# Attention of two heads at once in plain fp32 instead of one head at a time in split halves

## The chip, the cores and the metric

The kernel runs on one core of a Trainium2 chip, and the time is the device time of one execution in microseconds (us). A core has five engines with queues of their own: TensorE (PE in the profile: matrix multiplies; PEld are its weight loads, which run beside the multiplies), VectorE (DVE), ScalarE (ACT), GpSimd (POOL) and SyncE (SP, which issues most DMAs). They meet only through semaphores. Matrix products land in PSUM, eight banks of 128 partitions by 512 fp32 values.

## The reference

One decoder layer on a sequence of 512 tokens, model width 1024, all in float32: a norm, one wide input projection, a Mamba-2 scan over 16 heads and a forgetting attention over 16 heads side by side, an output projection, and a gated MLP. The change touches the attention alone:

```python
def fox_mixer(q, k, v, f_raw, f_bias, q_norm_w, k_norm_w):
    qh = rms_norm(heads(q), q_norm_w)          # 16 heads of 64
    kh = rms_norm(heads(k), k_norm_w)
    vh = heads(v)
    cum = jnp.cumsum(log_f, axis=1).transpose(0, 2, 1)
    for start in range(0, s, Q_BLOCK):         # blocks of 128 queries
        end = start + Q_BLOCK
        logits = jnp.einsum('bhqd,bhkd->bhqk', qh[:, :, start:end], kh[:, :, :end]) * scale
        logits = logits + cum[:, :, start:end, None] - cum[:, :, None, :end]
        p = jax.nn.softmax(jnp.where(causal, logits, -jnp.inf), axis=-1)
        outs.append(jnp.einsum('bhqk,bhkd->bhqd', p, vh[:, :, :end]))
```

## The kernel before

Large products keep fp32 accuracy by splitting: an operand is rounded to a type that TensorE takes in one pass (`F32R`, the "h" part), and what is left over is a second operand (the "l" part). `mm3` (L117) then adds three one-pass products, h·h, h·l and l·h. Rounding is an ACT copy (L110), the rest a DVE or POOL subtraction (L111). The input projections (rows named pw, pq, g), the output projection (po) and the MLP (up, Y, Z, X) are such products, and they are most of TensorE's work.

The attention works head by head, 16 heads of 64, as pairs of neighbouring heads that share the 128 columns of one transposed block.

- `v_proj` projects the values of four heads and keeps them split, 64 columns of h beside 64 columns of l (L533 on ACT, L534 on DVE).
- `fox_qk`, once for a pair, transposes q and k (L551). For each head it puts the h part of q over 64 partitions and the l part over the other 64 (`qs`); k gets its h part twice and its l part twice (`ks`), by ACT (L558) and DVE (L559). The copy on the other 64 partitions is made by ACT and DVE for the first pair (L561, L562) and by a DMA `ks<-ks` on SP's queue for the others.
- `fox_probs`, once for a head, fetches the row of cumulated gates by a DMA (`cum`), builds the bias with its causal mask in `bias` (ACT L584, POOL L586 and L589), and then for each of four query blocks adds two one-pass products over all 128 partitions (L599, L600; 128, 256, 384 and 512 columns), takes bias and row minimum in one DVE instruction (L601), the exponential on ACT (L605), and at the end scales the rows (L609).
- `fox_values`, once for a head, transposes the probabilities on TensorE in ten blocks (L626), splits them (ACT L628, DVE L629), and for each of four key blocks adds two one-pass products into one PSUM bank: h of the probabilities with all 128 columns of v, and l with 64 columns (L639). The two 64-partition halves of that bank are then added (ACT L643, DVE L644), and after a pair's second head the 128 rows are split for the output projection (L649, L650).

What sets the order: the loop at the end of the function calls these helpers head by head, with "fillers" between them (the projections of later heads and parts of the output projection). The attention's helpers run under `urgent()`, a priority that places their instructions early, and a scheduler puts the fillers' matmuls between them in each engine's queue. PSUM has three banks for the projections (`pg`), four for everything short-lived, scores and transposes included (`pm`), and one for the attention's output (`po`).

Of the kernel before, what the change touches and what calls it, by code (L numbers as in the profile page):

```python
# [15 lines left out]
P = 128  # L16
# [40 lines left out]
def tile_hybrid_layer(  # L57
# [468 lines left out]

    def v_proj(gi):
        tiles = token_block(wv[gi], "v%d" % gi)
        v = pa.tile([P, NTB, 4, 2 * HD], F32R, tag="v", name="v", bufs=2)
        for tb in range(NTB):  # L530
            c = (tb % 2) * 256
            o = tiles[tb // 2][:, c : c + 256].rearrange("p (h d) -> p h d", d=HD)
            act.activation(v[:, tb, :, 0:HD], o, AF.Copy, scale=r[:, tb : tb + 1])  # L533
            dve.scalar_tensor_tensor(  # L534
                out=v[:, tb, :, HD:], in0=o, scalar=r[:, tb : tb + 1], in1=raw(v[:, tb, :, 0:HD]),
                op0=ALU.mult, op1=ALU.subtract,
            )
        return v

    LO, HI = slice(0, HD), slice(HD, P)  # L540
    HALVES = ((LO, HI), (HI, LO))
    QOFF = (0, 128, 384, 768)

    def fox_qk(pair, tq, tk):
        qs = [pf.tile([P, SEQ], F32R, tag="qs", name="qs", bufs=4) for _ in range(2)]
        ks = [pf.tile([P, 2, SEQ], F32R, tag="ks", name="ks", bufs=4) for _ in range(2)]
        pr = pair % 2
        for tok, w in ((tk, kw), (tq, qw8)):
# [3 lines left out]
            for hd, (own, other) in enumerate(HALVES):  # L552
                src, sw = t[own, :], w[own]
                if tok is tq:
                    h, l = qs[hd][own, :], qs[hd][other, :]
                else:
                    h, l = ks[hd][own, 0, :], ks[hd][own, 1, :]
                act.activation(h, src, AF.Copy, scale=sw)  # L558
                dve.scalar_tensor_tensor(out=l, in0=src, scalar=sw, in1=raw(h), op0=ALU.mult, op1=ALU.subtract)  # L559
                if tok is tk and pair == 0:  # L560
                    act.activation(ks[hd][other, 0, :], src, AF.Copy, scale=sw)  # L561
                    dve.scalar_tensor_tensor(  # L562
                        out=ks[hd][other, 1, :], in0=src, scalar=sw, in1=raw(h), op0=ALU.mult, op1=ALU.subtract
                    )
                elif tok is tk:
                    nc.sync.dma_start(raw(ks[hd][other, :, :]), raw(ks[hd][own, :, :]))
        osum = pf.tile([P, SEQ], F32, tag="osum", name="osum", bufs=2)
        return qs, ks, osum

    def fox_probs(head, qs, ks):  # L570
# [4 lines left out]
        nm = pf.tile([P, NTB], F32, tag="nm", name="nm", bufs=2)  # L575
        sm = pf.tile([P, NTB], F32, tag="sm", name="sm", bufs=2)
        bias = pf.tile([P, 1280], F32, tag="bias", name="bias", bufs=2)
        prob = pf.tile([P, 1280], F32, tag="prob", name="prob", bufs=2)
        for qb in range(NTB):
            n = (qb + 1) * P  # L580
            b = bias[:, QOFF[qb] : QOFF[qb] + n]
# [7 lines left out]
            pool.affine_select(  # L589
                out=b[:, n - P :], in_=b[:, n - P :], pattern=[[-1, P]], compare_op=ALU.is_ge, fill=NEG, base=0,  # L590
                channel_multiplier=1,
            )
        for qb in range(NTB):
            n = (qb + 1) * P
            b = bias[:, QOFF[qb] : QOFF[qb] + n]
            p = prob[:, QOFF[qb] : QOFF[qb] + n]
            sps = mbank("S")
            qst = qs[:, qb * P : (qb + 1) * P]
            pe.matmul(sps[:, :n], qst, ks[:, 0, :n], start=True, stop=False)  # L599
            pe.matmul(sps[:, :n], qst, ks[:, 1, :n], start=False, stop=True)  # L600
            dve.tensor_tensor_reduce(  # L601
                out=p, in0=sps[:, :n], in1=b, scale=-1.0, scalar=-NEG, op0=ALU.add, op1=ALU.min,
                accum_out=nm[:, qb : qb + 1],
            )
            act.activation(p, p, AF.Exp, scale=-1.0, bias=nm[:, qb : qb + 1], accum_out=sm[:, qb : qb + 1])  # L605
        dve.reciprocal(sm, sm)
        for qb in range(NTB):
            p = prob[:, QOFF[qb] : QOFF[qb] + (qb + 1) * P]
            dve.tensor_scalar(out=p, in0=p, scalar1=sm[:, qb : qb + 1], scalar2=None, op0=ALU.mult)  # L609
        return prob  # L610

    def fox_values(head, prob, v, osum):
        lh = head % 4
        own, other = HALVES[head % 2]
        where = {}
        for n, kbs in enumerate(((0,), (1, 3), (2,))):
            w = sum(SEQ - kb * P for kb in kbs)
            t = mbank("pT")
            ph = pf.tile([P, w], F32R, tag="ph%d" % n, name="ph", bufs=2 if n == 0 else 1)
            pl = pf.tile([P, w], F32R, tag="pl%d" % n, name="pl", bufs=2 if n == 0 else 1)  # L620
            w = 0
            for kb in kbs:
                where[kb] = (ph, pl, w)
                for qb in range(kb, NTB):
                    o = QOFF[qb] + kb * P
                    pe.transpose(t[:, w : w + P], prob[:, o : o + P], ident)  # L626
                    w += P
            act.copy(ph, t[:, :w])  # L628
            dve.tensor_sub(pl, t[:, :w], raw(ph))  # L629
        o = po.tile([P, 512], F32, tag="o", name="o")  # L630
        for kb in range(NTB):
            ph, pl, w = where[kb]
            s = slice(w, w + SEQ - kb * P)
            cols = o[:, kb * P :]
            passes = ((P, slice(0, P), ph), (HD, slice(0, HD), pl))
            if kb == NTB - 1:
                passes = passes[::-1]
            for n, (m, vc, pt) in enumerate(passes):
                pe.matmul(  # L639
                    cols[:m], v[:, kb, lh, vc], pt[:, s], start=kb == 0 and n == 0, stop=kb == NTB - 1 and n == 1,  # L640
                    skip_group_check=True,
                )
        act.copy(osum[own, :], o[other, :])  # L643
        dve.tensor_add(osum[own, :], o[own, :], osum[own, :])  # L644
        if head % 2 == 0:
            return None
# [34 lines left out]
    def start_pair(p):  # L681
        with urgent():
            pairs[p] = fox_qk(p, *qk[p // 2])

    def start_head(n):
        qs, ks, _ = pairs[n // 2]
        with urgent():
            probs[n] = fox_probs(n, qs[n % 2], ks[n % 2])

    def end_head(n):  # L690
        with urgent():
            m = fox_values(n, probs.pop(n), vs[n // 4], pairs[n // 2][2])
        if m is not None:
            mf.append(m)

    fillers = {
        0: ["q1"], 3: ["v1"], 4: ["q2", "v2"], 5: ["o0"], 8: ["q3"], 9: ["a0", "o1"], 10: ["v3"], 12: ["o2"],
# [12 lines left out]
            out_proj((4 + g,), mf[2 * g : 2 * g + 2])  # L710

    start_pair(0)
    start_head(0)
    start_head(1)
    for n in range(16):
        for f in fillers.get(n, ()):
            fill(f)
        if n % 2 == 0 and n < 14:
            start_pair(n // 2 + 1)
        end_head(n)  # L720
        if n + 2 < 16:
            start_head(n + 2)
# [4 lines left out]
    nw = pf.tile([P, 1280], F32, tag="bias", name="nw", bufs=2)[:, :D]  # L727
    nc.sync.dma_start(nw, norm_ffn_w.to_broadcast([P, D]))
    for half in range(2):
        c = slice(half * 512, (half + 1) * 512)  # L730
        ks = slice(half * 4, half * 4 + 4)
        for tb in range(NTB):
            s = slice(tb * P, (tb + 1) * P)
            with urgent():
                xw = pf.tile([P, 512], F32, tag="osum" if tb % 2 else "cum", name="xw", bufs=2)
# [302 lines left out]
```

## Time and profile before

| what | value |
|---|---|
| timed runs | 805.68, 808.84, 808.51 us; median 808.51 |
| the profiled execution's own time | 806.18 us |
| its span | 804.4 us, granted TensorE clock 0.998 |
| DVE busy | 598.1 us (74%) |
| ACT busy | 438.6 us (55%) |
| POOL busy | 268.1 us (33%) |
| attention's stretch, first to last score and value product | about 221 to 438 us |

A row of the timeline gives the start, the duration, and with "x2" how many neighbouring instructions of one form were merged. TensorE works as a pipeline: a product lasts longer than the time until the next one starts. What a product costs a full queue is the step from its start to the next start, not its duration. `128*64` in a row is the number of rows and columns of the array that the product uses.

### The profile page before, as it was taken

What the parts mean: (1) busy time and instruction counts of PE and PEld (TensorE: products, weight loads), DVE (VectorE), ACT (ScalarE), POOL (GpSimd) and SP (SyncE); (2) the same over time, 40 slices, a digit from 0 to 9 for tenths busy, and PEclk for the clock granted to TensorE, in tenths of its full rate; (3) what the DMA queues carried; (4) which work ended last, traced back from release to release, by engine and by line L of the source; (5) the groups of instructions that cost most, each with busy time, mean ns of one, the idle gap of its engine ahead of it and who ended that gap; (6) DMA issues with size and microseconds to landing.
All of it is one profiled execution on the core that took longest, in us unless ns stands there. A gap on an engine that the chain in (4) does not pass through costs nothing.

```text
span 804.4 us, 11066 instructions
## 1 busy us (share of the span) xinstructions
PE 793.2 (99%) x3975; PEld 662.8 (82%) x3975; DVE 598.1 (74%) x949; ACT 438.6 (55%) x803; POOL 268.1 (33%) x266
## 2 busy tenths in 40 slices
PE   8999999999999999999999999999999999999997
PEld 6888877878989888888888888888888888888886
DVE  4797997588678789779796777667666766777744
ACT  7557645363588686685663554444443443556531
POOL 0004453643539147226310523333332233132120
PEclk9999999999999999999999999999999999999999
DMA  9615232331424243333330462232233233299983
GB/s 327 196 56 179 87 99 77 128 131 56 147 83 128 72 145 92 97 104 115 95 102 29 149 190 89 96 104 101 83 105 104 80 105 104 78 261 178 222 188 95
DMA packets 31399, 98.14 MB, mean 122 GB/s; under 512 B 4016, under 2 KB 5104, under 8 KB 31344
## 3 DMA queue, kind: packets, MB, share of 16 engines
q1 hardware_dynamic: 27456, 85.38, 32.1%
q0 software_dynamic: 3456, 11.54, 8.1%
q8 instruction: 31, 0.51, 0.3%
q10 hardware_dynamic: 432, 0.52, 0.2%
q14 instruction: 24, 0.20, 0.1%
HBM read 91.56 MB, written 2.20 MB: 117 GB/s over the span
## 4 chain that ended last, share of the span: by engine, by line
PE 89%; DVE 5%; DMA 2%; issue 2%; ACT 1%; POOL 1%; SPq 0%; DVEq 0%; POOLq 0%; ACTq 0%
PE up L117 30%; PE pw L117 15%; PE po L117 9%; PE Y L117 6%; PE g L117 5%; PE pq L117 4%; PE X L117 4%; PE Z L117 4%; PE o L639 2%; PE pT L626 2%; PE yd L458 2%; PE j L117 1%; PE S L600 1%; PE S L599 1%; DVE xs L397 1%
## 5 line engine op out<-in xcount | busy, mean ns | idle before, releaser
L110 ACT CAST wh<-wraw 128x1024 fp32r<-128x1024 f32 x103 | 108.2, 1052 | 121.6 <-PE up L117 79.3
L117 PE MATMUL up<-hh,wh 128*128 128x512 f32 (+1 forms) x360 | 138.6, 386 | 0.0
L117 PE MATMUL up<-hl,wh 128*128 128x512 f32 (+1 forms) x360 | 138.5, 385 | 0.0
L117 PE MATMUL up<-hh,wl 128*128 128x512 f32 (+1 forms) x360 | 138.3, 384 | 0.0
L111 DVE TENSOR_TENSOR wl<-wraw,wh 128x1024 fp32r<-128x1024 f32 x83 | 109.0, 1314 | 20.8 <-ACT wh L110 19.0
L117 PEld LDWEIGHTS up<-hl,wh 128*128 128x128 f32 x360 | 67.6, 188 | 13.7 <-issue 0.2
L117 PEld LDWEIGHTS up<-hh,wh 128*128 128x128 f32 x360 | 67.5, 188 | 13.6 <-issue 0.2
L117 PEld LDWEIGHTS up<-hh,wl 128*128 128x128 f32 x360 | 67.6, 188 | 13.3
L117 PE MATMUL pw<-wh,xh 128*128 128x512 f32 x192 | 77.3, 407 | 0.0
L117 PE MATMUL pw<-wl,xh 128*128 128x512 f32 x192 | 76.0, 396 | 0.0
L117 PE MATMUL pw<-wh,xl 128*128 128x512 f32 x192 | 75.8, 396 | 0.0
L831 DVE TENSOR_TENSOR up<-up,R 128x512 f32<-128x512 f32 x44 | 30.3, 692 | 59.5 <-PE up L117 59.5
L111 POOL TENSOR_TENSOR wl<-wraw,wh 128x1024 fp32r<-128x1024 f32 x20 | 50.2, 2511 | 60.9 <-ACT wh L110 60.9
L836 DVE SCALAR_TENSOR_TENSOR ua<-up,pc,ua 128x511 f32<-128x511 f32 (+1 forms) x88 | 66.3, 758 | 1.4
L605 ACT ACTIVATE prob<-prob,nm 128x384 f32<-128x384 f32 (+2 forms) x64 | 35.9, 562 | 29.3 <-DVE nm L601 29.2
L792 ACT CAST wh<-T 128x1024 fp32r<-128x1024 f32 (+1 forms) x30 | 29.3, 977 | 36.9 <-PE Z L117 15.3
L793 DVE TENSOR_TENSOR wl<-T,wh 128x1024 fp32r<-128x1024 f32 (+1 forms) x30 | 33.8, 1134 | 19.2 <-ACT wh L792 18.8
L586 POOL TENSOR_SCALAR bias<-cum,tokS 128x256 f32<-128x256 f32 (+1 forms) x32 | 21.4, 678 | 77.5 <-DVE nm L601 67.5
L846 POOL TENSOR_TENSOR ua<-ua 128x512 f32<-128x512 f32 x11 | 15.0, 1365 | 92.5 <-DVE ua L836 92.5
L117 PEld LDWEIGHTS pw<-wh,xh 128*128 128x128 f32 x192 | 36.1, 188 | 7.3 <-issue 0.5
L117 PEld LDWEIGHTS pw<-wl,xh 128*128 128x128 f32 x192 | 36.2, 188 | 7.2 <-issue 0.7
L117 PEld LDWEIGHTS pw<-wh,xl 128*128 128x128 f32 x192 | 36.0, 188 | 7.3
(241 smaller groups left out, 2004.3 us busy)
## 6 DMA issues: line engine op xcount, KB each, us to landing
wraw<-in_wup_dram SPq DMA_DIRECT2D x44, 512.0 KB, 3.3
T<-in_wdown_dram POOLq DMA_DIRECT2D x20, 512.0 KB, 7.7
wraw<-in_wqk_dram SPq DMA_DIRECT2D x16, 512.0 KB, 3.3
wraw<-in_wout_dram SPq DMA_DIRECT2D x16, 512.0 KB, 3.4
wraw<-in_wxbc_dram SPq DMA_DIRECT2D x11, 512.0 KB, 5.5
wraw<-in_wdown_dram SPq DMA_DIRECT2D x10, 512.0 KB, 3.6
T<-in_wdown_dram SPq DMA_DIRECT2D x10, 512.0 KB, 5.6
wraw<-in_wz_dram SPq DMA_DIRECT2D x8, 512.0 KB, 3.2
```

What stands on the lines that cost most here:

```text
L110: act.copy(h, r)
L111: (sub or dve).tensor_tensor(out=l, in0=r, in1=raw(h), op=ALU.subtract)
L117: ins = pe.matmul(o, a, b, start=start and n == 0, stop=stop and n == 2, **kw)
L458: pe.matmul(yd[:, h * HD : (h + 1) * HD], sc[:, h, :], xdt[:, h * HD : (h + 1) * HD], start=True, stop=True)
L586: pool.tensor_scalar(out=b, in0=cum[:, :n], scalar1=-1.0, scalar2=edge, op0=ALU.mult, op1=ALU.add)
L605: act.activation(p, p, AF.Exp, scale=-1.0, bias=nm[:, qb : qb + 1], accum_out=sm[:, qb : qb + 1])
L626: pe.transpose(t[:, w : w + P], prob[:, o : o + P], ident)
L639: pe.matmul(cols[:m], v[:, kb, lh, vc], pt[:, s], start=kb == 0 and n == 0, stop=kb == NTB - 1 and n == 1, skip_group_check=True,)
L792: act.copy(h[:, :n], src[:, :n])
L793: dve.tensor_tensor(out=l[:, :n], in0=src[:, :n], in1=raw(h[:, :n]), op=ALU.subtract)
L831: dve.tensor_mul(xp, o, R2)
L836: dve.scalar_tensor_tensor(out=a[:, s:], in0=xp[:, : SEQ - s], scalar=pc[:, cw + 2 - s : cw + 3 - s], in1=a[:, s:], op0=ALU.mult, op1=ALU.add,
```

## The change

Both heads of a pair are now worked on together, and nothing in the attention is split before its result. The values stay whole, 64 columns a head. `fox_qk` makes one fp32 tile of q and one of k, with the pair's first head on partitions 0 to 63 and its second on 64 to 127. `fox_bias` builds the bias inside the tile that later holds the probabilities. `fox_scores` issues for each query block one fp32 product of 64 rows for each head, into two banks. `fox_turn` transposes the probabilities and copies them once, unsplit. `fox_values` adds, for both heads, fp32 products of 64 columns into one bank, the first head on its partitions 0 to 63 and the second on 64 to 127. The loop starts a pair's scores for both heads in one step, turns each head in its place, and ends a pair after its second head. The core of the diff:

```diff
 def v_proj(gi):
-        v = pa.tile([P, NTB, 4, 2 * HD], F32R, tag="v", name="v", bufs=2)
...
-            dve.scalar_tensor_tensor(
-                out=v[:, tb, :, HD:], in0=o, scalar=r[:, tb : tb + 1], in1=raw(v[:, tb, :, 0:HD]),
+        v = pa.tile([P, NTB, 4, HD], F32, tag="v", name="v", bufs=2)
...
+                act.activation(v[:, tb], o, AF.Copy, scale=r[:, tb : tb + 1])
 def fox_qk(pair, tq, tk):
-        qs = [pf.tile([P, SEQ], F32R, tag="qs", name="qs", bufs=4) for _ in range(2)]
-        ks = [pf.tile([P, 2, SEQ], F32R, tag="ks", name="ks", bufs=4) for _ in range(2)]
...
-                elif tok is tk:
-                    nc.sync.dma_start(raw(ks[hd][other, :, :]), raw(ks[hd][own, :, :]))
+            f = pf.tile([P, SEQ], F32, tag=tag, name=tag, bufs=2)
+            act.activation(f, t, AF.Copy, scale=w)
+    def fox_scores(q, k, both):
...
+            sps = [mbank("S") for _ in range(2)]
+            for o, rows in zip(sps, HEADS):
+                pe.matmul(o[:, :n], q[rows, qb * P : (qb + 1) * P], k[rows, :n], start=True, stop=True)
-            pe.matmul(sps[:, :n], qst, ks[:, 0, :n], start=True, stop=False)
-            pe.matmul(sps[:, :n], qst, ks[:, 1, :n], start=False, stop=True)
...
-            act.copy(ph, t[:, :w])
-            dve.tensor_sub(pl, t[:, :w], raw(ph))
+            act.copy(pt, t[:, :w])
...
+            for i, rows in enumerate(HEADS):
+                pt, w = turned[i][kb]
                 pe.matmul(
-                    cols[:m], v[:, kb, lh, vc], pt[:, s], start=kb == 0 and n == 0, stop=kb == NTB - 1 and n == 1,
+                    o[rows, kb * P :], v[:, kb, (2 * pair + i) % 4, :], pt[:, w : w + SEQ - kb * P],
+                    start=kb == 0, stop=kb == NTB - 1, skip_group_check=True,
...
-        act.copy(osum[own, :], o[other, :])
-        dve.tensor_add(osum[own, :], o[own, :], osum[own, :])
...
-        act.copy(mh, osum)
-        dve.tensor_sub(ml, osum, raw(mh))
+        act.copy(mh, o)
+        dve.tensor_sub(ml, o, raw(mh))
```

The scheduler's order moves with it. First, TensorE's queue where scores are made. Before, at the first two heads (`S_2046` is the last block of head 0, `S_2078` to `S_2088` are blocks of head 1, `pw` is a filler):

```order
L599 MATMUL S_2046<-ks_1984,qs_1982 128x512 [waits DVE_49]
L599 MATMUL S_2078<-ks_1985,qs_1983 128x128 [waits DVE_49,Activation_49]
L600 MATMUL S_2078<-ks_1985,qs_1983 128x128
L599 MATMUL S_2083<-ks_1985,qs_1983 128x256 [waits DVE_49]
L600 MATMUL S_2083<-ks_1985,qs_1983 128x256
L600 MATMUL S_2046<-ks_1984,qs_1982 128x512
L117 MATMUL pw_2187<-wh_2109,xh_93 128x512
L599 MATMUL S_2088<-ks_1985,qs_1983 128x384 [waits DVE_49]
L600 MATMUL S_2088<-ks_1985,qs_1983 128x384
```

Now, at the second pair: the two small blocks of both heads (`S_2280` and `S_2288` of the first head, `S_2281` and `S_2289` of the second) between two fillers.

```order
L117 MATMUL pw_2161<-wh_2100,xh_93 128x512
L582 MATMUL S_2280<-k_2236,q_2229 128x128 [waits DVE_49,Activation_49]
L582 MATMUL S_2281<-k_2236,q_2229 128x128 [waits DVE_49]
L582 MATMUL S_2288<-k_2236,q_2229 128x256 [waits PE_49]
L582 MATMUL S_2289<-k_2236,q_2229 128x256 [waits PE_49]
L117 MATMUL pw_2161<-wl_2101,xh_93 128x512
```

The four large products follow after sixteen fillers, again as one group:

```order
L117 MATMUL pw_2161<-wh_2136,xl_94 128x512
L582 MATMUL S_2296<-k_2236,q_2229 128x384 [waits DVE_49]
L582 MATMUL S_2297<-k_2236,q_2229 128x384 [waits DVE_49]
L582 MATMUL S_2304<-k_2236,q_2229 128x512 [waits DVE_49]
L582 MATMUL S_2305<-k_2236,q_2229 128x512 [waits DVE_49]
L117 MATMUL pw_2160<-wh_2136,xh_93 128x512
```

What moved: two products into one bank became one product in each of two banks, and a pair's eight score products stand in two groups of four, the heads in turn. Each row of the new kernel is an fp32 product.

Second, TensorE's queue where the values of the first pair are made (`pt_2330` and `pt_2337` are blocks of head 0, `pt_2349` and `pt_2356` of head 1; the pair's first three products, two of 512 columns and one of 384, stand ahead of it, the first of them alone between fillers):

```order
L117 MATMUL pq_2490<-wh_2548,xh_93 128x256
L619 MATMUL o_2360<-pt_2349,v_1969 64x384 [waits Activation_49]
L619 MATMUL o_2360<-pt_2337,v_1969 64x256
L619 MATMUL o_2360<-pt_2356,v_1969 64x256 [waits Activation_49]
L619 MATMUL o_2360<-pt_2330,v_1969 64x128
L619 MATMUL o_2360<-pt_2349,v_1969 64x128
L117 MATMUL pq_2490<-wl_2549,xh_93 128x256
```

What moved: the products with the l part are gone, and products of the two heads stand next to each other where one head's two products stood.

Third, DVE's queue between the scaling of one head's rows and the next pair's scores. Before (heads 2 and 3 are prepared while head 0 is turned):

```order
L609 TENSOR_SCALAR prob_2061<-prob_2061,sm_2059 128x512
L559 SCALAR_TENSOR_TENSOR qs_2251<-qkT_2266,qw8_205,qs_2251 64x512 [waits Activation_49]
L559 SCALAR_TENSOR_TENSOR ks_2254<-qkT_2255,pc_74,ks_2254 64x512 [waits Activation_49]
L629 TENSOR_TENSOR pl_2278<-pT_2276,ph_2277 128x512 [waits Activation_49]
L111 TENSOR_TENSOR wl_2613<-wraw_2610,wh_2612 128x1024 [waits DMAHW5_49,Activation_49]
L559 SCALAR_TENSOR_TENSOR qs_2252<-qkT_2266,qw8_205,qs_2252 64x512 [waits Activation_49]
L629 TENSOR_TENSOR pl_2287<-pT_2285,ph_2286 128x512 [waits Activation_49]
L515 TENSOR_REDUCE ms_2104<-sq_2238 128x2x4 [waits Activation_49]
L601 ISA prob_2317,nm_2314<-S_2334,bias_2316 128x128 [waits PE_49,Pool_49]
```

And now:

```order
L596 TENSOR_SCALAR prob_2013<-prob_2013,sm_2033 128x512
L515 TENSOR_REDUCE ms_2077<-sq_2153 128x2x4 [waits Activation_49]
L515 TENSOR_REDUCE ms_2077<-sq_2157 128x2x4 [waits Activation_49]
L585 ISA prob_2240,nm_2276<-S_2280,prob_2240 128x128 [waits PE_49,Pool_49]
L585 ISA nm_2276 128x1
L585 ISA prob_2259,nm_2277<-S_2281,prob_2259 128x128 [waits PE_49,Pool_49]
```

What moved: DVE's subtractions for q, k and the probabilities are gone, and the reductions of the two heads alternate.

More of the change, by code (lines that the diff above doesn't have):

```diff
@@ L551, in fox_qk, with fox_bias @@
                 pe.transpose(t[:, tb * P : (tb + 1) * P], tok[:, tb, pr * P : (pr + 1) * P], ident)
[L552 to L564, printed above, removed]
-                elif tok is tk:
-                    nc.sync.dma_start(raw(ks[hd][other, :, :]), raw(ks[hd][own, :, :]))
-        osum = pf.tile([P, SEQ], F32, tag="osum", name="osum", bufs=2)
-        return qs, ks, osum
-    def fox_probs(head, qs, ks):
+            f = pf.tile([P, SEQ], F32, tag=tag, name=tag, bufs=2)
+            act.activation(f, t, AF.Copy, scale=w)
+            both.append(f)
+        return both
+    def fox_bias(head):
         cum = pf.tile([P, SEQ], F32, tag="cum", name="cum", bufs=2)
@@ L574, in fox_probs @@
         )
[L575 to L578, printed above, removed]
+        prob = pf.tile([P, 1280], F32, tag="prob", name="prob", bufs=4)
         for qb in range(NTB):
             n = (qb + 1) * P
-            b = bias[:, QOFF[qb] : QOFF[qb] + n]
+            b = prob[:, QOFF[qb] : QOFF[qb] + n]
             edge = tokS[:, 1, qb, 16 + head : 17 + head]
@@ L726, in tile_hybrid_layer @@
     hl = pxt.tile([P, NK, SEQ], F32R, tag="xl", name="hl")
-    nw = pf.tile([P, 1280], F32, tag="bias", name="nw", bufs=2)[:, :D]
+    nw = pf.tile([P, 1280], F32, tag="prob", name="nw", bufs=4)[:, :D]
     nc.sync.dma_start(nw, norm_ffn_w.to_broadcast([P, D]))
@@ L734, in tile_hybrid_layer @@
             with urgent():
[L735 removed]
+                xw = pf.tile([P, 512], F32, tag="xw" if tb % 2 else "cum", name="xw", bufs=2)
                 (dve if (half, tb) == (1, 3) else pool).tensor_tensor(out=xw, in0=x2[:, tb, c], in1=nw[:, c], op=ALU.mult)
```

92 lines of the change are left out of this document (41 added, 51 removed).

## The prediction

> **What bounds the kernel now.** I read the page first: its busy line, the granted clock over the span, and the chain of work that ended last.
>
> ```profile
> PE 793.2 (99%) x3975; PEld 662.8 (82%) x3975; DVE 598.1 (74%) x949; ACT 438.6 (55%) x803; POOL 268.1 (33%) x266
> PEclk9999999999999999999999999999999999999999
> PE 89%; DVE 5%; DMA 2%; issue 2%; ACT 1%; POOL 1%; SPq 0%; DVEq 0%; POOLq 0%; ACTq 0%
> ```
>
> TensorE is busy 99% of the span at a full clock, and 89% of the chain is TensorE's own work. So an edit is worth what it adds to or takes from TensorE's queue; work taken off DVE, ACT or a DMA is worth only the waits of TensorE that it ends. Whether "busy" hides slack in the attention's stretch is the next question, and the table by stage and the list of TensorE's waits there (205 to 470 us) answer it.
>
> ```profile
> 205.00:221.00 16.00, 16.00 (x111) 14.85 (x110) 9.66 (x16) 10.20 (x18) 8.30 (x14) 1.00 0.39 138
> 300.00:340.00 40.00, 38.86 (x234) 33.93 (x233) 35.25 (x82) 26.96 (x63) 22.12 (x28) 1.00 0.31 97
> PE S L599 <- DMA ks<-ks: 1.4, 1, 1.4
> PE po L117 <- DVE v L534: 1.1, 1, 1.1
> PE pT L626 <- DVE ks L559: 0.8, 1, 0.8
> PE po L117 <- DVE x L263: 0.3, 1, 0.3
> ```
>
> TensorE is the first number after each stretch's length: even in the attention's worst 40 us it stands idle 1.14 us. In the whole stretch it waits four times, 3.6 us in all, and the first three waits, 3.3 us, are for things that the change deletes. That is the most that the relief of the other engines can bring directly. The rest is decided by what a product costs in TensorE's queue.
>
> **The old products.** One head's eight value products stand together once, in TensorE's timeline near 437 us.
>
> ```profile
> 436.38 0.40 PE L639 MATMUL o<-ph,v 128*128 128x512 f32 x1
> 436.62 0.40 PE L639 MATMUL o<-pl,v 128*64 128x512 f32 x1
> 436.85 0.34 PE L639 MATMUL o<-ph,v 128*128 128x384 f32 x1
> 437.03 0.34 PE L639 MATMUL o<-pl,v 128*64 128x384 f32 x1
> 437.20 0.28 PE L639 MATMUL o<-ph,v 128*128 128x256 f32 x1
> 437.32 0.34 PE L639 MATMUL o<-pl,v 128*64 128x256 f32 x2
> 437.50 0.28 PE L639 MATMUL o<-ph,v 128*128 128x128 f32 x1
> 437.61 0.45 PE L117 MATMUL po<-wh,msl 128*128 128x512 f32 x1
> ```
>
> From 436.38 to the next product at 437.61 is 1.23 us a head. The scores have the same eight sizes, and their steps agree where the two largest stand together:
>
> ```profile
> 245.33 0.39 PE L599 MATMUL S<-ks,qs 128*128 128x512 f32 x1
> 245.56 0.40 PE L600 MATMUL S<-ks,qs 128*128 128x512 f32 x1
> 245.79 0.28 PE L117 MATMUL pq<-wh,xl 128*128 128x256 f32 x1
> ```
>
> That is 0.46 us for two products of 512 columns, 0.23 us each, as for the values. So scores and values cost 1.23 us a head each, 2.46 us a pair each.
>
> **The new products.** The scan has plain fp32 products; the view of one line and the timeline show what they are.
>
> ```profile
> L471 PE MATMUL st<-xdt,b_tok x12: 591/592/667, 92.3 to 194.5; 128*128 128x512 f32 x12
> L450 PE MATMUL cb<-cT,bT x16: 270/275/356, 63.5 to 195.3; 128*128 128x128 f32 x16
> 92.34 1.02 PE L471 MATMUL st<-xdt,b_tok 128*128 128x512 f32 x2
> 93.20 0.38 PE L450 MATMUL cb<-cT,bT 128*128 128x128 f32 x2
> ```
>
> The code issues six `st` and eight `cb`, and the trace has 12 and 16: an fp32 product is two passes. Two of 512 columns take 1.02 us, one lasts 0.592, so a pass costs 1.02 - 0.59 = 0.43 us; of 128 columns, 0.38 - 0.275 = 0.105 us. On the line between them 256 columns cost 0.21 and 384 cost 0.32. The four sizes sum to 1.07 us a pass, 2.13 us a head, 4.26 us a pair, for scores and values each. So plain fp32 costs 1.80 us a pair more than the split, if nothing else changes: 2 x 1.80 x 8 = **+28.8 us**. That is one end.
>
> **Two heads in one array.** The other end depends on whether products that use different halves of the array run at the same time: scores use 64 rows each, values 64 columns each. No product of the old kernel leaves room for another, so no row shows it. What the rows do show is what holds a product: not the end of the one before (0.39 us), only its stream through the array (0.23 us). A product on other rows or columns shares no stream, so I take it that it may start beside the one before, but in the order of the queue. That order costs something. The queue holds a1 a2 b1 b2 (two passes of head a, then of head b). a2 must wait for a1; b1 starts with a2; b2 starts with the next a1. A group of two sizes s and t then takes 2s + 3t in place of 4s + 4t. The score groups of the new order are (128, 256) and (384, 512): 2 x 0.105 + 3 x 0.21 = 0.84 and 2 x 0.32 + 3 x 0.43 = 1.93, together 2.77 us a pair against 2.46: +0.31.
>
> For the values the order gives, at a typical pair, 512 alone (0.86); 512 with 384 (a pass of 0.43, then two of 0.32: 1.07); and 384, 256, 256, 128, 128 in turn, where the same rule gives 1.27. Together 3.20 against 2.46: +0.74. Eight pairs: 8 x (0.31 + 0.74) = **+8.4 us**. So even with both halves busy the plain product loses, because its two passes at half pace are only half covered by the other head.
>
> Lower still would be two heads fully abreast, 2.13 us a pair: 8 x 2 x (2.13 - 2.46) = -5.3 us. Between these ends (-5.3, +28.8) I take +8.4.
>
> The Trainium skill (TensorEngine Tiling (Array Packing), Key Properties) says that a change of tiling mode drains TensorE. The rows at 436.62 and 436.85 speak against it for columns: going from `128*128` to `128*64` and back costs 0.23 us a step, as without a change. For rows no run here shows it. By that rule the sum would be higher by about 0.16 us a switch (0.59 lasting less 0.43 of stream), 32 switches for the scores, 5 us; I leave it to a rival.
>
> **The other engines.** DVE loses the subtractions of q, k and the probabilities and the addition of the halves:
>
> ```profile
> L559 DVE SCALAR_TENSOR_TENSOR ks<-qkT,pc,ks x16: 730/750/758, 213.0 to 404.4; 64x512 fp32r<-64x512 f32 x16
> L629 DVE TENSOR_TENSOR pl<-pT,ph x48: 403/678/694, 239.3 to 432.4; 128x512 fp32r<-128x512 f32 x32, 128x256 fp32r<-128x256 f32 x16
> L644 DVE TENSOR_TENSOR osum<-o,osum x16: 670/688/696, 252.6 to 438.4; 64x512 f32<-64x512 f32 x16
> L534 DVE SCALAR_TENSOR_TENSOR v<-pq,r,v 128x256 fp32r<-128x256 f32 x16 | 7.5, 478 | 3.2 <-ACT v L533 3.1
> ```
>
> With the same count for `qs` that is 32 x 0.75 + 32 x 0.68 + 16 x 0.41 + 16 x 0.69 + 7.5 = about 71 us, and SP's queue loses the 14 DMAs `ks<-ks`. All of it lay beside TensorE's work, so it is worth the waits above, at most 3.3 us. What ACT gets is cheaper than what it loses: one copy of q and of k a pair over 128 partitions for four over 64. The bias moves ahead of the scores of a whole pair and is off the path as long as it stays a pair ahead.
>
> One wait is new in kind. A pair's first four scores fill all four short-lived banks, so the next four wait for DVE's reductions of the first four. Behind them on TensorE stand the fillers, and everything behind those. Sixteen fillers at 0.23 us, 3.7 us, lie between; the four reductions are small:
>
> ```profile
> L601 DVE CUSTOM_DVE_ANT_0 prob<-S,bias x64: 271/480/692, 222.9 to 419.4; 128x128 f32<-128x128 f32 x16, 128x256 f32<-128x256 f32 x16, 128x384 f32<-128x384 f32 x16, 128x512 f32<-128x512 f32 x16
> ```
>
> at most four of 0.48 us, 1.9 us. If DVE stands 2 us behind, the cover is gone and each us more costs a us, eight times over. I book -2 us for the waits: 3.3 saved, 1.3 given back; the ends are -3.3 and +4.
>
> **The sum.** 806.18 (the profiled execution: span 804.4 and 1.8 around it) + 8.4 - 2 = 812.6. The median of the runs shown is 2.3 us above the profiled one, and they spread over 3 us, so I add 1.4 and predict **814 us**.
>
> **Rivals.**
>
> 1. *No overlap at all.* The fp32 passes of two heads follow one another. For it: every pair of products in the trace does. Against it: none of them leaves half the array free. 806.2 + 28.8 - 2 + 1.4 = 834 us. Chance 0.28.
> 2. *Only rows or only columns overlap.* Rows only: 806.2 + 8 x (0.31 + 1.80) - 2 + 1.4 = 822.5; columns only: 806.2 + 8 x (1.80 + 0.74) - 2 + 1.4 = 826. Chance 0.13.
> 3. *Overlap, but TensorE empties at each change of the tile's shape.* 32 changes at the scores and 0.16 us each: 814 + 5 = 819; with the values' 48 changes as well, 827. For it: nothing measured; against it: the rows at 436.62 and 436.85. Chance 0.08. This is the skill's rule above.
> 4. *Not slower: the heads run fully abreast.* If TensorE starts b1 beside a1, a pair's products take one head's 2.13 us: 806.2 - 5.3 - 3.3 + 1.4 = 799 us. It decides as soon as the second head's first pass need not wait for the first head's second; below a mean of 2.46 us a pair the change gains. Against it: in every timeline row above, products start in the order issued. The Trainium skill (TensorE: Matmul & The Clock Gate, Part 3, measured speedup vs the span model) gives packed products about the time of one; taken at its word it is this rival, though its section also says that products start and end in order. No run here shows packed products. Chance 0.06.
>
> **How the numbers follow.** My forecast has 0.45. Its own range is 809 to 819: the waits from -3.3 to +4, and the spread of the runs. The range for all cases must reach to the serial case and may leave out the abreast one (0.06), the upper part of the serial one (0.11) and little else: 807 to 835. A measurement of this kernel can tell about 0.5%, 4 us, from no change. Faster by more needs rival 4: 0.05. Within 4 us lie the lower fifth of my forecast and a remainder of rival 4: 0.10. Slower: 0.85.
>
> **What would show it.** In the new timeline, score and value passes of the two heads with starts closer than 0.43 us at 512 columns mean overlap; steps of 0.43 us throughout mean rival 1. A gap of 0.16 us at the edges of the score groups means rival 3. The three waits named above should be gone from TensorE's list, DVE's busy time should fall by about 70 us, and the span after the attention should be what it was. I am wrong in kind if TensorE's idle time grows past some 5 us (a new wait), or if an fp32 product of 64 rows or columns isn't two passes.

## The result and the profile after

| | kernel before | kernel after |
|---|---|---|
| median of four runs each, us | 808.10 (805.68 to 808.84) | 818.15 (816.74 to 819.24) |
| ratio after / before, 95% interval | | 1.0129 [1.0102, 1.0156] |
| profiled execution, us (span) | 806.18 (804.4) | 817.79 (816.0) |
| first `qkT` product to the last product of the program, us | 587.7 | 598.4 |

The changed kernel is slower by 1.3%, some 10 us. The forecast was 814 us with a range of 807 to 835 and slower as the likeliest sign: sign and range held, and the size came out some 4 us above. Two of its reasons didn't hold, and the rest of this document is about them.

The page of the kernel after: first the busy line, then the granted clock, then the shares of the chain that ended last.

```profile
PE 807.8 (99%) x3975; PEld 648.2 (79%) x3975; DVE 528.8 (65%) x835; ACT 414.2 (51%) x769; POOL 263.4 (32%) x266
PEclk9999999999999999999999999999999999999999
PE 95%; DVE 3%; DMA 1%; issue 0%; SPq 0%; ACT 0%; DVEq 0%; ACTq 0%
```

The relief came as planned: DVE has 69.3 us less (598.1 to 528.8), and TensorE's share of the chain rose from 89% to 95%. In the worst 40 us of before, TensorE's busy time (the first number behind the stretch's length) now fills the stretch, and of TensorE's waits behind the start of the attention one small one is left, long after it:

```profile
300.00:340.00 40.00, 40.00 (x246) 30.66 (x245) 24.19 (x57) 24.36 (x58) 22.55 (x28) 1.00 0.29 93
```

```profile
PE up L117 <- DVE up L807: 0.4, 1, 0.4
```

So the 10 us are no wait of TensorE: they are time in its own queue. TensorE's timeline (start, length, engine and product, xcount of passes) shows a whole group of large scores between fillers of 512 columns. A merged row carries the shape of its first product, so that the x8 here are four passes of 384 columns and four of 512:

```profile
224.33 0.39 PE L117 MATMUL pw<-wl,xh 128*128 128x512 f32 x1
224.65 1.77 PE L582 MATMUL S<-k,q 64*128 64x384 f32 x8
226.35 0.51 PE L117 MATMUL pw<-wh,xl 128*128 128x512 f32 x1
226.70 0.39 PE L117 MATMUL pw<-wh,xh 128*128 128x512 f32 x1
```

From 224.33 to 226.70 there are 2.37 us. Two fillers of 0.23 us are in it, so the group costs 1.91 us. Its eight passes in turn would take 4 x 0.32 + 4 x 0.43 = 3.00 us; the two heads fully abreast would take 1.50. So the heads do overlap, and 0.41 us is lost somewhere. A window of the same timeline 8 ns wide, set on the group's first instant, shows the overlap itself:

```profile
224.65 0.59 PE L582 MATMUL S<-k,q 64*128 64x384 f32 x2
```

Two passes are under way, and both begin and end within 0.59 us, the length of one. The loss stands at the edges. The first score pass comes 0.32 us behind the start of the filler ahead of it (224.33 to 224.65) where a step is 0.23: 0.09 lost. The weight loads of the fillers behind the group show another part:

```profile
226.35 0.19 PEld L117 LDWEIGHTS pw<-wh,xl 128*128 128x128 f32 x1 [0.76 <-issue]
226.46 0.19 PEld L117 LDWEIGHTS pw<-wh,xh 128*128 128x128 f32 x1
226.70 0.19 PEld L117 LDWEIGHTS pw<-wl,xh 128*128 128x128 f32 x1
```

The filler that starts at 226.70 had its weights loading from 226.46, beside the product ahead of it. The filler at 226.35 starts together with its own load: that load could not be brought forward, and the step to the next filler is 0.35 instead of 0.23, 0.11 lost. The same two losses come once on the way in (there the first head's two passes of 384 columns start 0.42 us apart, at 224.65 and 225.08, in place of 0.32) and once on the way out, which makes the 0.41.

The small score group and a value group where one head stands alone show the same:

```profile
236.07 0.39 PE L117 MATMUL pw<-wh,xh 128*128 128x512 f32 x1
236.39 0.93 PE L582 MATMUL S<-k,q 64*128 64x128 f32 x8
237.25 0.50 PE L117 MATMUL pw<-wl,xh 128*128 128x512 f32 x1
237.58 0.39 PE L117 MATMUL pw<-wh,xl 128*128 128x512 f32 x1
```

```profile
284.34 0.39 PE L117 MATMUL pw<-wh,xl 128*128 128x512 f32 x1
284.66 1.07 PE L619 MATMUL o<-pt,v 128*64 128x512 f32 x2
285.66 0.87 PE L609 MATMUL pT<-ident,prob 128*128 128x128 f32 x6
```

1.51 less two fillers is 1.06 us where 0.63 would be abreast: 0.43 lost, much the same. The lone value product has no partner, so nothing overlaps; yet its first pass is 0.09 late as well. The second of the six transposes behind it starts at 285.83, so it costs 285.83 - 284.34 - 0.23 - 0.11 = 1.15 us, where its two passes stream for 0.86. The next group of this pair, at 286.79, has a product of 384 columns of the other head beside one of 512; it costs 1.15 as well, so the partner is free. And the group of five value products:

```profile
310.21 0.28 PE L117 MATMUL pq<-wh,xh 128*128 128x256 f32 x1
310.41 1.51 PE L619 MATMUL o<-pt,v 128*64 128x384 f32 x10
311.85 0.39 PE L117 MATMUL pq<-wl,xh 128*128 128x256 f32 x1
312.08 0.28 PE L117 MATMUL pq<-wh,xl 128*128 128x256 f32 x1
```

312.08 - 310.21 is 1.87, less two fillers of 0.12: 1.63 us. One head has 384, 256 and 128 columns in it, two passes each, 1.27 us; the other only 256 and 128. The longer head plus 0.36 is what the group takes.

From here on a **trip** is the way from whole-array products to half-array products and back, and two theories compete. *A*: each half of the array runs its own sequence, so that a group costs the longer head's own passes, and each trip costs 0.3 to 0.4 us more. *B*: the rule of the prediction, b1 starts with a2 in the order of the queue, and trips cost nothing. B gives the large score group 1.93 and the small one 0.84. A has 1.91 and 1.06, but its trip was read from these very rows; the runs below test it. The large group alone cannot tell the two apart.

### The profile page after: what moved, and what is told of

Same layout as the page of the kernel before. It is cut to its first block, busy times and chain, and to the rows that moved or that the text cites. A ratio compares the mean times of both kernels' runs of the same rounds, so it can differ in the third digit from the quotient of the medians.

```text
span 816.0 us, 10856 instructions
## 1 busy us (share of the span) xinstructions
PE 807.8 (99%) x3975; PEld 648.2 (79%) x3975; DVE 528.8 (65%) x835; ACT 414.2 (51%) x769; POOL 263.4 (32%) x266
## 4 chain that ended last, share of the span: by engine, by line
PE 95%; DVE 3%; DMA 1%; issue 0%; SPq 0%; ACT 0%; DVEq 0%; ACTq 0%
PE up L117 29%; PE pw L117 16%; PE po L117 11%; PE pq L117 6%; PE Y L117 6%; PE g L117 5%; PE X L117 4%; PE Z L117 4%; PE o L619 3%; PE S L582 3%; PE pT L609 2%; PE yd L458 1%; PE j L117 1%; DVE xs L397 1%; PE qkT L546 1%; PE yo L464 1%
## 5 line engine op out<-in xcount | busy, mean ns | idle before, releaser
L117 PEld LDWEIGHTS up<-hh,wh 128*128 128x128 f32 x360 | 67.6, 188 | 14.1 <-PE up L117 0.8
L111 POOL TENSOR_TENSOR wl<-wraw,wh 128x1024 fp32r<-128x1024 f32 x20 | 48.5, 2424 | 87.7 <-ACT wh L110 87.7
L263 DVE TENSOR_TENSOR x<-po,x 128x512 f32<-128x512 f32 x48 | 32.6, 685 | 30.4 <-PE po L117 30.4
L589 ACT ACTIVATE prob<-prob,nm 128x128 f32<-128x128 f32 (+3 forms) x64 | 35.3, 553 | 28.9 <-DVE nm L585 28.7
L585 DVE CUSTOM_DVE_ANT_0 prob<-S,prob 128x128 f32<-128x128 f32 (+3 forms) x64 | 28.0, 487 | 33.1 <-PE S L582 29.6
L117 PEld LDWEIGHTS pw<-wh,xl 128*128 128x128 f32 x192 | 36.1, 188 | 10.7 <-issue 3.4
```

The lines of the kernel that those rows point to most:

```text
L111: (sub or dve).tensor_tensor(out=l, in0=r, in1=raw(h), op=ALU.subtract)
L117: ins = pe.matmul(o, a, b, start=start and n == 0, stop=stop and n == 2, **kw)
L263: dve.tensor_add(dst, banks[tb], dst)
L585: dve.tensor_tensor_reduce(out=p, in0=sps[i][:, :n], in1=p, scale=-1.0, scalar=-NEG, op0=ALU.add, op1=ALU.min, accum_out=nm[i][:, qb : qb ...
L589: act.activation(p, p, AF.Exp, scale=-1.0, bias=nm[i][:, qb : qb + 1], accum_out=sm[i][:, qb : qb + 1])
```

## The experiments

The ratios are to the kernel before, timed on the same chip beside each (medians 808.10 beside after, 806.57 beside the next four rows and 806.99 beside heads in turn, split groups, both together and values only, together). The column "cost" is worked out from the starts in each trace: for each group of score and value products, the time from the start of the step ahead of it to the start of the second step behind it, less a normal step for these two (0.226 us for a filler of 512 columns, 0.120 for 256, 0.109 for a transpose), summed over the program. Waits that stand at a group are in it. Where a single step lies between two groups, its delay counts in both, up to 1.1 us of a total. "Stretch" is the time from the first `qkT` product to the last product. A group is not always one trip: the old split products make none, and in split groups the added transpose breaks nine of the 44 groups in two, which makes 53 trips.

| kernel | ratio, 95% interval | groups | cost, us | stretch, us |
|---|---|---|---|---|
| before | 1 | 82 | 44.2 | 587.7 |
| after | 1.0129 [1.0102, 1.0156] | 38 | 54.9 | 598.4 |
| scores only | 1.0040 [1.0023, 1.0057] | 51 | 47.2 | 591.0 |
| values only | 1.0068 [1.0047, 1.0090] | 55 | 49.6 | 592.3 |
| whole array | 1.0323 [1.0295, 1.0350] | 44 | 70.3 | 612.6 |
| values together | 1.0071 [1.0049, 1.0093] | 29 | 50.7 | 593.7 |
| heads in turn | 1.0183 [1.0160, 1.0206] | 44 | 60.4 | 603.2 |
| split groups | 1.0211 [1.0189, 1.0232] | 44 | 62.2 | 604.9 |
| both together | 1.0003 [0.9988, 1.0017] | 24 | 45.3 | 588.2 |
| values only, together | 0.9946 [0.9927, 0.9966] | 49 | 41.3 | 583.9 |

The stretch follows the cost to within 1.3 us in every kernel. From before to after both grow by 10.7 us: what TensorE spends at the score and value products is the whole loss.

### Whole array: no overlap, no trips

Zeros are added to q and v so that every product takes all 128 rows and columns.

```
-                pe.matmul(o[:, :n], q[rows, qb * P : (qb + 1) * P], k[rows, :n], start=True, stop=True)
+                pe.matmul(o[:, :n], qh[:, qb * P : (qb + 1) * P], k[:, :n], start=True, stop=True)
...
-                    o[rows, kb * P :], v[:, kb, (2 * pair + i) % 4, :], pt[:, w : w + SEQ - kb * P],
-                    start=kb == 0, stop=kb == NTB - 1, skip_group_check=True,
+                    o[:, kb * P :], v[:, kb, (2 * pair + i) % 4, :], pt[:, w : w + SEQ - kb * P],
+                    start=kb == 0 and i == 0, stop=kb == NTB - 1 and i == 1, skip_group_check=True,
```

(`qh` is a head's q with the other head's 64 rows zero; `v` has 128 columns a head, half of them zero.)

> The changed kernel with each head's q padded by zeros to 128 rows and each head's v padded by zeros to 128 columns: the same fp32 passes over the whole array, so no two can run at the same time and the tile's shape never changes. Theory A: 8 x 2 x 4.26 = 68.2 us of attention products against the 54.7 us that they and their changes of shape take in the changed kernel: +13.5 us on the changed kernel, about 831 us. If overlap were worth nothing: the changed kernel's time less its changes of shape (38 groups of about 0.37 us, 14 us), about 804 us. My rival of no overlap said 834.

TensorE's timeline at the same group:

```profile
226.56 0.40 PE L117 MATMUL pw<-wh,xh 128*128 128x512 f32 x1
226.80 3.17 PE L594 MATMUL S<-k,q 128*128 128x384 f32 x8
229.40 0.79 PE L117 MATMUL pw<-wl,xh 128*128 128x512 f32 x1
230.03 0.39 PE L117 MATMUL pw<-wh,xl 128*128 128x512 f32 x1
```

230.03 - 226.56 - 0.46 = 3.01 us, and 3.00 is the sum of eight passes: the heads stand in turn, and the edges cost nothing (226.56 to 226.80 is a plain step; the filler at 229.40 is recorded as starting 0.03 us behind the last score pass, and its step of 0.63 makes up for that). Here too the fillers are split products and the scores plain fp32 ones, so the change of type alone is not what costs 0.41. The kernel takes 832.88 us, 3.2% over before, near the 834 of the prediction's first rival. This is what the change would cost if halves did not overlap; that they do is worth some 15 us net of the trips.

### Scores alone, values alone

Each takes one half of the change into the kernel before: the new `fox_qk`, `fox_bias` and `fox_scores` with the old values, or the new `v_proj`, `fox_turn` and `fox_values` with the old scores.

In scores alone, against before:

```
-            pe.matmul(sps[:, :n], qst, ks[:, 0, :n], start=True, stop=False)
-            pe.matmul(sps[:, :n], qst, ks[:, 1, :n], start=False, stop=True)
+            for o, rows in zip(sps, HEADS):
+                pe.matmul(o[:, :n], q[rows, qb * P : (qb + 1) * P], k[rows, :n], start=True, stop=True)
```

In values alone, against before:

```
-                    cols[:m], v[:, kb, lh, vc], pt[:, s], start=kb == 0 and n == 0, stop=kb == NTB - 1 and n == 1,
+                    o[rows, kb * P :], v[:, kb, (2 * pair + i) % 4, :], pt[:, w : w + SEQ - kb * P],
+                    start=kb == 0, stop=kb == NTB - 1, skip_group_check=True,
```

> The score half of the change alone; values as before. Theory A (the two heads' passes start together, and each change between the whole array and a half-array tile costs about 0.2 us, seen as 1.06 and 1.91 us for the two score groups of a pair in the changed kernel's trace): scores 8 x 2.97 = 23.8 us against the 21.7 us that they take before, waits for the k copies and for DVE's q and k subtractions gone (0.8 us more): +1.3 us on before, 0.0 to +3. Theory B (my prediction's rule: overlap only as far as the queue's order allows, changes of shape free): 8 x 0.31 less 2.2 us of waits: +0.3. The two hardly differ here; the run says how much of the +10 us belongs to the scores. If it is above +6, both have the scores wrong.

> The value half of the change alone; scores as before. Theory A: the value products of the changed kernel's trace take 30.9 us in all against 19.5 us before, less one wait of 1.1 us: +10 us on before (+8 to +12), so that nearly all of the loss is here. Theory B: 8 x 0.74 less 1.1: +4.8. If the two halves do not add up to the whole change (about +10), they hinder each other.

Scores alone cost 0.40%, values alone 0.68%: together 1.08%, against 1.29 for the whole change, whose interval holds that. Both halves lose, the values more. Scores alone lost 3.2 us where A had 1.3 (0 to 3) and B 0.3, since the scheduler broke four of the eight large score groups: three in two, at some 1.05 and 1.26 us in place of 1.91, and one in three. Values alone lost 5.5 us, outside A's 8 to 12 and nearer to B's 4.8; but TensorE's waits in the attention, 3.6 us in before, are none here (A had booked only 1.1 of them), and the value products cost some 29 us where the old ones come to 8 x 2.46 = 19.7, a difference of some 9. The 30.9 us that A's sum gives for the values of after had taken every score group as whole; by the table's count they take 29.7, and the scores 25.2. The total thus tells the theories apart badly, the groups tell them apart well: the small score group, whole in all eight pairs of scores alone, takes 1.06 us there too, A's figure and not B's 0.84.

### Split groups: one more trip in each score group

A transpose of the identity, 128 by 128, is put between the two sizes of each score group; it writes to a bank that the score product behind it overwrites. It adds 0.11 us of its own and one trip.

```
+            if qb % 2:
+                tc.keep_in_program_order(pe.transpose(sps[0][:, 0:P], ident, ident))
             for o, rows in zip(sps, HEADS):
...
+                if qb % 2:
+                    tc.keep_in_program_order(ins)
```

> The changed kernel with one small product over the whole array (a 128x128 transpose of the identity, 0.11 us, overwritten by the score after it) put between the two sizes of each score group: 16 more trips from half-array tiles to the whole array and back. Theory A: each costs 0.4 us and its own 0.11: 16 x 0.51 = +8 us on the changed kernel, about 825 on a kernel before of 807, with gaps of about 0.09 us and exposed weight loads of 0.107 us at each side. If changes of shape are free (theory B): +1.8 us.

TensorE's timeline where the large group was:

```profile
242.94 0.40 PE L117 MATMUL pw<-wl,xh 128*128 128x512 f32 x1
243.27 0.92 PE L584 MATMUL S<-k,q 64*128 64x384 f32 x4
244.11 0.50 PE L117 MATMUL pw<-wh,xl 128*128 128x512 f32 x1
244.45 0.27 PE L582 MATMUL S<-ident 128*128 128x128 f32 x1
244.66 1.13 PE L584 MATMUL S<-k,q 64*128 64x512 f32 x4
245.71 0.50 PE L117 MATMUL pw<-wh,xh 128*128 128x512 f32 x1
246.05 0.40 PE L117 MATMUL pw<-wl,xh 128*128 128x512 f32 x1
```

A filler went in beside the transpose. Without the transpose's own 0.11 the pieces cost 1.06 and 1.26 us where the group cost 1.91: 0.41 more for the second trip. At the small sizes the two pieces together cost 1.41 in place of 1.06, 0.35 more. By the two ratios the time rose by 0.82% of 807 on after, 6.6 us, where B had 1.8 and A 8. By the table's cost it is 7.3, of which 16 transposes make 1.8 and 15 more trips (53 for 38) the other 5.5, 0.37 us each. The trip is real and has its price.

### Heads in turn: the queue's order

One head's two products of a group are issued before the other's: a a b b in place of a b a b.

```
+                for i, rows in enumerate(HEADS):
+                    for b in (qb, qb + 1):
+                        m = (b + 1) * P
+                        ins = pe.matmul(
+                            ahead[b][i][:, :m], q[rows, b * P : (b + 1) * P], k[rows, :m], start=True, stop=True
+                        )
+                        if i or b > qb:
+                            tc.keep_in_program_order(ins)
```

> The changed kernel, but in a score group both products of one head stand ahead of both of the other (a a b b, not a b a b). Theory A (each half of the array runs its own sequence, whatever the order in the queue): the first passes of the two heads still start within 10 ns of each other, the whole groups take the 1.06 and 1.91 us of the changed kernel, and the time is the changed kernel's within 2 us where the scheduler leaves the groups whole (about 817 on a kernel before of 807). Theory B (a pass starts only after the one ahead of it in the queue has started): b waits for a's second product, 1.05 and 2.57 us plus the changes of shape in place of 0.84 and 1.93: +6.8 us.

Where a group stayed whole, the timeline reads as after, although head b's first pass has four passes of head a ahead of it in the queue. The second fence is a window 20 ns wide at the group's first instant:

```profile
325.97 0.40 PE L117 MATMUL po<-wh,mfl 128*128 128x512 f32 x1
326.30 1.78 PE L587 MATMUL S<-k,q 64*128 64x384 f32 x8
328.01 0.50 PE L117 MATMUL po<-wh,mfh 128*128 128x512 f32 x1
328.35 0.39 PE L117 MATMUL po<-wl,mfh 128*128 128x512 f32 x1
```

```profile
326.30 0.60 PE L587 MATMUL S<-k,q 64*128 64x384 f32 x2
```

2.38 - 0.46 = 1.92 us, where B had 2.57, and two passes begin within the 20 ns. They can't be two of one head (those keep at least 0.32 us between them), so b's first pass went past three of a's. The order of the queue does not hold a half back for the other: this refutes the rule "b1 starts with a2" on its own. The Trainium skill (TensorE: Matmul & The Clock Gate, Part 3, the mechanism) has products starting and ending strictly in program order; between halves of the array, this trace does not. The kernel is slower all the same, for another reason, which the timeline of another pair shows:

```profile
241.47 0.40 PE L117 MATMUL pw<-wl,xh 128*128 128x512 f32 x1
241.80 0.91 PE L587 MATMUL S<-k,q 64*128 64x384 f32 x2
242.64 0.50 PE L117 MATMUL pw<-wh,xl 128*128 128x512 f32 x1
242.97 0.40 PE L117 MATMUL pw<-wh,xh 128*128 128x512 f32 x1
243.30 1.77 PE L587 MATMUL S<-k,q 64*128 64x512 f32 x6
245.01 0.50 PE L117 MATMUL pw<-wl,xh 128*128 128x512 f32 x1
```

The scheduler sent a lone product ahead: 384 columns of one head, 1.04 us with its trip, and then the rest, which still costs 1.91. Four pairs of eight have this, and two pairs have their group of five value products broken in two, so that there are 44 groups where after has 38. By the ratios the kernel is 4.4 us slower than after, between A's 0 (for whole groups) and B's 6.8: the total doesn't decide here, the whole groups do.

### Values together, both together

All eight value products of a pair stand in one group, the heads in turn; what is ready last leads. In "both together" the scores are pinned as well, the larger size and head 1 first.

```
-        for kb in range(NTB):
-            for i, rows in enumerate(HEADS):
+        for n, kb in enumerate((2, 0, 1, 3)):
+            for i, rows in reversed(list(enumerate(HEADS))):
...
-                    start=kb == 0, stop=kb == NTB - 1, skip_group_check=True,
+                    start=n == 0, stop=n == NTB - 1, skip_group_check=True,
                 )
+                if n or not i:
+                    tc.keep_in_program_order(ins)
```

> The changed kernel with a pair's eight value products kept next to each other, equal sizes of the two heads side by side (the last pair of the changed kernel stands so already, and takes 2.50 us). Theory A: 8 x 2.50 = 20.0 us in place of 30.9: -10 us on the changed kernel, about 808 us (806 to 811). Theory B (overlap by the order of the queue, changes of shape free): 2.24 us a pair in place of 3.20: -7.7, about 810.5. If grouping were without effect: 818.

> The changed kernel with both score groups and value groups kept whole (the run values_together had five lone products of 512 columns, a head without its partner, at 1.25 us each). Theory A: scores 8 x 2.97 = 23.8, values 20.0, 43.8 us against 41.2 before, less about 3 us of waits: the kernel before within 2 us, some 6 us less than values_together. If something else than products and changes of shape held the changed kernel back: no better than values_together, +0.7%.

The values came out as A has it, in TensorE's timeline:

```profile
253.71 0.28 PE L117 MATMUL pq<-wh,xl 128*128 128x256 f32 x1
253.91 2.38 PE L619 MATMUL o<-pt,v 128*64 128x256 f32 x16
256.22 0.39 PE L117 MATMUL pq<-wh,xh 128*128 128x256 f32 x1
256.44 0.28 PE L117 MATMUL pq<-wl,xh 128*128 128x256 f32 x1
```

256.44 - 253.71 - 0.24 = 2.49 us, which is 2.13 fully abreast and one trip of 0.36, against 1.15 + 1.17 + 1.63 = 3.95 for the three groups of after. But by the ratios the time fell by 4.7 us on after, not by the 10 expected of A: with the values moved, the scheduler broke the scores, and five lone products of 512 (1.25 each; after has one) and two lone ones of 384 stand in the trace. With the scores pinned as well ("both together") the missing half came: cost 45.3 (A had 43.8; one of the 16 score groups still broke in three), and a time of 807.64, not to be told from before. So the loss of the change is given back by grouping and order alone, with the same products.

### Values alone, together

The old split scores with the new values in one group.

> The value half alone, as in the run values_only, but a pair's eight value products kept next to each other, equal sizes side by side; scores split as before. Theory A: values 8 x 2.50 = 20.0 us against 19.5 before and 28.8 in values_only; DVE's relief ends the 1.1 us wait for v: -1 us on before (-3 to +1), 8 us less than values_only. Theory B: 8 x 2.24 = 17.9: -3 us on before.

It is faster than either theory had it: 802.57, ratio 0.9946 [0.9927, 0.9966], 4.4 us below before, where A had 1 (at most 3) and B 3. Its eight value groups cost 2.50 us each, A's figure and not B's 2.24; they make 20.0, where the prediction's 2.46 a pair made 19.7 of the old ones, so the products themselves gain nothing. What it gains is the waits; TensorE's list for the attention now reads

```profile
PE po L117 <- DVE x L263: 0.3, 1, 0.3
PE S L596 <- DMA ks<-ks: 0.2, 1, 0.2
```

0.5 us in place of 3.6. That is 3.1 of the 4.4 us (0.54% of 807). The stretch is shorter by 3.8, so 0.7 more lies in it; neither that nor the rest of the 1.3 can I place.

## Why the prediction was right in size and wrong in two steps

- **What bounds the kernel.** Right. TensorE's queue set the time in all ten kernels, and the time followed the cost of its products.
- **The old products, 2.46 us a pair.** About right: 16 x 2.46 = 39.4 us; the trace's 44.2 has two of the three named waits in it (1.4 and 1.1 us, and some 0.5 more beside them), so 41 to 42 without them.
- **The new products' passes** (0.105, 0.21, 0.32, 0.43 us; two a product). Right, also for half an array: in the whole-array kernel they add up without a remainder.
- **Two heads in one array: "b1 starts with a2", in the order of the queue.** Wrong, and this is the step that failed. A half of the array runs its own sequence; the heads start together, and the queue's order between them does not matter (heads in turn). The rule was too dear: 2.77 us a pair for the scores, where abreast is 2.13.
- **The change of shape at nothing** (rival 3, chance 0.08). Wrong too, in the other direction. A trip costs some 0.4 us at the scores and 0.29 to 0.37 at the values. The rows at 436.62 and 436.85, on which I dismissed it, are of split products with an fp32r type; these did not pay for `128*64`, but a plain fp32 product of 64 columns does (284.34 to 284.66 is 0.32 us in place of 0.23). The evidence was of another kind of product. The Trainium skill (TensorEngine Tiling (Array Packing), Key Properties) has a change of tiling mode drain TensorE. The 0.09 us agrees with a wait at each change; a full emptying these rows don't show, for the filler at 226.35 starts ahead of the recorded end of the last score pass (226.42, an end that the profile models). My 0.16 us a switch came near the 0.2 measured by luck: half of the 0.2 is the late weight load, of which the 0.16 knew nothing.
- **The sum of both.** Scores: forecast 2.77 us a pair, measured 1.06 + 1.91 = 2.97. Values: forecast 3.20, measured 3.95 at six of the eight pairs. There the heads' work is uneven, so the rule was only 0.21 too dear (by A the longer heads take 0.86 + 0.86 + 1.27 = 2.99), and three trips of 0.32 stand against that. Over the program, after's groups hold 40.8 us of the longer head; the 14.1 left of 54.9 make 0.37 us for each of the 38 trips. The forecast had 8 x (2.77 + 3.20) = 47.8: 7.0 too much by the rule, and 14.1 of trips at nothing. So the term of +8.4 measured +13 to +14 (54.9 less 41 to 42). Rival 4's mechanism (abreast) and rival 3's (a price for the change of shape) were both at work, and no single case of mine had the two together. That the total fell near the forecast is in part luck: the two errors have opposite signs, and how far they cancel depends on the sizes of this kernel's groups.
- **The waits, -2.** The three named waits went (3.3 us), none came in the attention, 0.4 us came far behind it. The new wait that I feared, four scores that hold all short-lived banks, does not show: nothing of TensorE's idle time is left there. So -3.3, and the 1.3 that I booked against it did not come.
- **DVE, about -70.** Measured -69.3.
- **The span after the attention**, which should have been what it was. Wrong as a sign: from the last value product to the last product of the program it is 367.2 us in place of 361.9. Behind that product stand 74 `po` fillers where before had 52; 22 at 0.23 us are 5.1 of the 5.3 us. They moved, and are no loss: the whole stretch grows with the cost of the products alone.
- **The sum.** +13 to +14 less 3.3 is about +10 to +10.7; the stretch grew by 10.7, where +6.4 was forecast (+8.4 - 2). The medians differ by 10.05; the profiled executions by 11.6, of which 1.0 lies ahead of the attention, where the change touches nothing.

Not settled: which part of the array's hardware makes a pair of halves wait for the whole. And 0.09 us of gap is told from 0.11 us of exposed weight load by starts alone; no run changed the one without the other.

## What to carry to other kernels

In these traces a group of plain fp32 products on half of the array costs what the longer of the two halves' sequences costs, plus a trip of 0.3 to 0.4 us each time TensorE goes there and back. So count the groups in the scheduled queue before counting columns, keep the halves' work equal within a group, and pin the group: the scheduler broke unpinned score groups in after and in several of the runs. Pinning did not hold them all: 15 of 16 score groups stayed whole in "both together", 11 of 16 in heads in turn. Evidence for what an edge costs must come from products of the same type: the split ones did not show what plain fp32 pays. Where two unknown costs of opposite sign stand in a forecast, a rival with both in it belongs on the list; a total that agrees proves neither.

## What was not expected of the hardware

- Products on different halves overtake one another in the queue, by up to three passes in the heads-in-turn kernel; the two heads' first passes start 5 to 14 ns apart.
- In these traces a weight load is not brought forward across a change between whole and half array: the product there starts together with its load, and the next step is late by 0.11 us for 128 columns (after, 226.35).
- A half-array product without a partner still pays the trip: 1.15 us for two passes of 512 columns that stream for 0.86.
